# Output-weight pieces: gate row kept on chip, split inside the raw tile, one store per piece

## The chip, the cores and the metric

The kernel runs on 1 core of one Trainium2 chip. The metric is the device time of one execution in microseconds (us), as the median of several runs. TensorE (PE) does the matmuls, VectorE (DVE), ScalarE (ACT) and GpSimd (POOL) work beside it, and every transfer of this stage is issued from the queue of SyncE (SP). Each engine, and SP too, takes its instructions strictly in the order in which they stand in its program: one that waits holds up all behind it.

## The reference

One layer of a trunk over 2048 latent positions with 256 context positions, in float32. What the change touches is the weight of the output projection and its gate:

```
ada = jnp.einsum('bd,lde->lbe', jax.nn.silu(c), w_ada) + b_ada[:, None, :]
sh1, sc1, g1, sh2, sc2, g2 = (m[:, None, :] for m in jnp.split(ada[l], 6, axis=-1))
h = modulate(rmsnorm(x, norm_mix[l]), sh1, sc1)
o, _, _ = token_mixers(h @ w_in[l], lb_f, lb_b, first, hf_c, hb_c, *mix_args)
x = x + g1 * (o @ w_out[l])
h2 = modulate(rmsnorm(x, norm_ffn[l]), sh2, sc2)
x = x + g2 * conv_ffn(h2, w_up[l], conv_w[l], conv_b[l], w_down[l], rows)
return rmsnorm(x, norm_final)
```

`w_out` is 1024 x 1024 and `g1` has 1024 elements. The kernel multiplies the columns of `w_out` by `g1` ahead of time, so that the output projection is a plain product. The token mixers are a gated recurrence of 4 heads in two directions and a spatial gate of 4 heads.

## The kernel before

**Stages.** The input projection and the mixers run first, in two halves of 1024 positions each (about 50 to 540 us and 540 to 1000 us of the profiled execution). The output projection and the second norm follow, then the up-projection with its convolution and the down-projection. float32 products are made of three products of rounded halves ("hi" and "lo", type float32r): `split` (line 128) copies a tile to its rounded hi half on ACT (line 131) and subtracts that from the tile on DVE or POOL to get the lo half (line 132).

**Banks of the input projection.** `run_banks` walks over blocks of 128 columns of `w_in`. For each block and each 512 positions, 24 matmuls fill one PSUM bank `pj`. The block's weights come in by `load_raw` (line 213, 512 KB into a `raw` tile), ACT casts them to `whi`, and POOL (or DVE) subtracts to `wlo`. The inputs are `xh` and `xl`. At the middle, between the two halves, 16 loads of 512 KB (lines 1048 and 1049) bring in the second half's `xh` and `xl`, each as soon as PE has last read the piece that it overwrites. The first three blocks of the second half are called here the first block (the recurrence's output gate, evicted through `sig` and `sgt`), the second block (values, evicted to `vv`) and the third block (queries, evicted through `sig` and `qs`).

**Heads.** The work of a head runs beside the next head's banks: DVE makes `Q` (line 758), POOL makes `kd` (755), PE makes the scores `sc` (line 65), then seven levels follow each other, each with a masked copy (781), an update of `Q` (481), of the keys `K` on DVE and POOL (557) with copies on ACT (559), and of the totals `tot` (488).

**Output weights.** `w_out_ops` (lines 917 to 932) is a generator in a queue of background work. `Pump` steps it when a rough count of PE time has passed what it yielded, so the yields space its pieces: 5.0 between a piece's loads and its arithmetic, 2.5 after its stores. There are 16 pieces of 128 x 512. Each takes a `raw` tile of 128 x 1024: the weight goes into its first half (line 924), the gate's row, broadcast to 128 partitions, into its second (line 925). DVE multiplies (928), ACT casts to the hi half in a tile `wo_hi` of its own, of which there is one (`acc`, shared with other work), DVE subtracts into the half that held the gate, and two transfers store hi and lo to `wo_d` in HBM (930, 931). `raw` has 3 buffers, which these pieces share with `load_raw` and, later, with `w_down_ops`.

**Order.** Outside a few stretches a scheduler (Tile) places the instructions on each engine's queue by its own estimate of when each can run; `pin` keeps an instruction at its place in the order in which the program was written.

Of the kernel before, what the change touches and what calls it, by code (L numbers as in the profile page):

```python
# [9 lines left out]
F32 = mybir.dt.float32  # L10
F32R = mybir.dt.float32r
# [7 lines left out]
P = 128  # L19
D = 1024  # L20
NK = D // P
# [62 lines left out]
def tile_trunk(ctx, tc, x, c, cx, c_ctx, w_ada, b_ada, norm_mix, norm_ffn, w_in, hg_norm, sgu_g, sgu_b,  # L84
               w_sp, b_sp, w_out, w_up, conv_w, conv_b, w_down, norm_final, masks, out):
    nc = tc.nc
    V, S, G, T = nc.vector, nc.scalar, nc.gpsimd, Tensor(nc.tensor)
    ld = nc.sync.dma_start
    st = nc.sync.dma_start
    pin = tc.keep_in_program_order  # L90
# [22 lines left out]
    g_d = dr.tile([2, D], F32, name="g_d")  # L113
# [3 lines left out]
    wo_d = dr.tile([P, NK, 2, D], F32, name="wo_d")  # L117
# [11 lines left out]
    def split(hi, lo, raw, eng=None, keep=lambda i: i):  # L129

        keep(S.copy(hi, raw))  # L131
        (eng or G).tensor_sub(lo, raw, hi.bitcast(F32))  # L132
# [56 lines left out]
    with es1:  # L189
        ps = es1.enter_context(tc.tile_pool(name="ps1", bufs=1, space=PSUM, reuse_waits="tile"))  # L190
        p1 = es1.enter_context(tc.tile_pool(name="p1", bufs=1, reuse_waits="tile"))
        pm = es1.enter_context(tc.tile_pool(name="pm", bufs=1, reuse_waits="tile"))
# [13 lines left out]
        def raw_tile():  # L206
            return p1.tile([P, D], F32, tag="raw", name="raw", bufs=3)
# [52 lines left out]
        acc = ph.tile([P, 2, 512], F32, tag="S", name="acc")  # L260
# [655 lines left out]

        def w_out_ops():

            for k in range(NK):
                for n in range(2):  # L920
                    cl = slice(n * 512, n * 512 + 512)
                    raw = raw_tile()
                    w, g = raw[:, :512], raw[:, 512:]
                    ld(w, w_out[k * P:(k + 1) * P, cl])
                    ld(g, g_d[0:1, cl].broadcast_to([P, 512]))
                    yield 5.0
                    hi = pm.tile([P, 512], F32, tag="acc", name="wo_hi")
                    V.tensor_mul(w, w, g)
                    split(hi.bitcast(F32R), g.bitcast(F32R), w, V)
                    st(wo_d[:, k, 0, cl], hi)  # L930
                    st(wo_d[:, k, 1, cl], g)
                    yield 2.5

        def w_down_ops():
# [20 lines left out]
        def head(hh, h):  # L955
# [18 lines left out]
            def pre_g():  # L974
                if prev[0] >= 0:
                    need(hg_q, (prev[0], prev[1], "keys"))
                else:
                    need(bg_q, "x1")
                    for e in range(8):
                        bg_q.add(ada_block(e))  # L980
                    bg_q.add(w_out_ops())
                    bg_q.add(conv_taps())
                    bg_q.add(w_down_ops())
                t["F"] = pk.tile([P, 2, TH], F32, tag="F", name="F", align_bytes=AL)
                t["K"] = pk.tile([P, 2, TH], F32, tag="K", name="K", bufs=2, align_bytes=AL)
# [130 lines left out]
    def ubank():  # L1116
        return ps2.tile([P, 512], F32, tag="up", name="up", bufs=4)
# [363 lines left out]
    for n, (u, i) in enumerate(prods):  # L1481
# [4 lines left out]
        p = ubank()  # L1486
        hi, lo = u.A[i]
# [34 lines left out]
    V = Kept(nc.vector, pin)  # L1522
# [243 lines left out]
```

## Time and profile before

| what | before |
|---|---|
| median of 3 runs | 2491.28 us (2486.34 to 2496.11) |
| profiled execution, its own time | 2488.51 us |
| its span from first to last instruction | 2486.7 us |
| mean granted PE clock | 0.996 |
| busy share of the span: PE / DVE / ACT / POOL | 97% / 72% / 39% / 43% |
| mean DMA rate over the span | 161 GB/s |

Times in the text are microseconds from the start of the span. A row of the timeline has the start, the duration, the engine, the line, the operation, `out<-in`, and in brackets how long the engine sat idle before it and what ended that. Instructions that follow each other and are alike are merged into one row with their count.

### The profile page before, as it was taken

The page shows a single profiled execution, that of the slowest core. Times are in us where ns is not written, and L with a number is a line of the kernel's source. Part 1 is how long each engine was busy: PE and PEld are TensorE (multiplying, and loading weights), DVE is VectorE, ACT ScalarE, POOL GpSimd, SP SyncE. Part 2 cuts the span into 40 slices and gives each one's busy share as a digit, 9 for nine tenths or more (in the row PEclk, how much of TensorE's full clock was granted, in tenths as well). Part 3 has the DMA queues.
Part 4 walks back from the last instruction along what each step waited for, and adds up shares of the span by engine and source line. Part 5 has one row for each costly group of instructions (what it writes and reads, how often), then busy time and mean ns, then how long its engine had stood idle before and what let it go on. Part 6 is the DMA issues. An engine that isn't in the chain of part 4 may idle for free.

```text
span 2486.7 us, 32820 instructions
## 1 busy us (share of the span) xinstructions
PE 2423.9 (97%) x11859; PEld 2014.4 (81%) x11859; DVE 1793.6 (72%) x2375; ACT 963.8 (39%) x1607; POOL 1059.7 (43%) x871
## 2 busy tenths in 40 slices
PE   7999999999999999999999999999999999999998
PEld 4787888788888888788778888878878888888887
DVE  5866875646765856465699778759999993685876
ACT  2554334433344443245443333324333342433343
POOL 1444232232333433100587887878878770000002
PEclk9999999999999999999999999999999999999999
DMA  8355445573353422768832222372222239834745
GB/s 296 97 189 188 126 138 188 175 261 115 106 179 127 148 98 86 241 207 260 299 103 91 89 87 90 132 282 84 84 86 91 91 100 349 306 126 149 228 148 195
DMA packets 307838, 400.13 MB, mean 161 GB/s; under 512 B 33105, under 2 KB 216137, under 8 KB 304605
## 3 DMA queue, kind: packets, MB, share of 16 engines
q1 hardware_dynamic: 304420, 397.30, 47.9%
q8 instruction: 94, 1.54, 0.3%
q10 hardware_dynamic: 3257, 0.75, 0.1%
q14 instruction: 67, 0.55, 0.1%
HBM read 288.85 MB, written 109.13 MB: 160 GB/s over the span
## 4 chain that ended last, share of the span: by engine, by line
PE 38%; DVE 7%; issue 3%; ACT 1%; POOL 1%; DMA 1%; SPq 0%; POOLq 0%; ACTq 0%; DVEq 0%
PE up L65 24%; PE dn L65 14%; DVE dn L1343 3%; DVE edges L1348 1%; DVE gp L1419 1%; ACT dn L1340 0%; DMA yf<-yd 0%; POOL ra L1625 0%; POOL rr L1626 0%; POOL Al L132 0%; DVE keep L1413 0%; DMA xn<-cv 0%; DVE keep L1429 0%; ACT cv L1362 0%; ACT Ah L131 0%
## 5 line engine op out<-in xcount | busy, mean ns | idle before, releaser
L1343 DVE SCALAR_TENSOR_TENSOR dn<-gp,taps,dn 128x1024 f32<-128x1024 f32 x352 | 448.9, 1282 | 21.0 <-ACT dn L1340 17.8
L65 PE MATMUL up<-yf,Ah 128*128 128x512 f32 x1232 | 394.7, 390 | 2.7 <-DMA yf<-yd 2.7
L132 POOL TENSOR_TENSOR Al<-raw,Ah 128x512 fp32r<-128x512 f32 x264 | 344.4, 1313 | 92.6 <-ACT Ah L131 87.5
L65 PE MATMUL dn<-thl,mhl 128*128 128x512 f32 x1680 | 381.5, 390 | 1.2 <-ACT thl L131 1.2
L65 PEld LDWEIGHTS dn<-thl,mhl 128*128 128x128 f32 x1680 | 315.3, 188 | 67.4 <-ACT thl L131 2.0
L65 PE MATMUL pj<-xh,whi 128*128 128x512 f32 x896 | 364.9, 408 | 0.5 <-ACT xh L131 0.5
L65 PE MATMUL pj<-xl,whi 128*128 128x512 f32 x896 | 351.7, 393 | 1.9 <-DVE xl L132 1.1
L65 PE MATMUL pj<-xh,wlo 128*128 128x512 f32 x896 | 351.7, 393 | 1.0 <-DVE wlo L132 1.0
L65 PE MATMUL up<-xah,Al 128*128 128x512 f32 x704 | 275.9, 392 | 2.0 <-POOL Al L132 1.8
L65 PE MATMUL up<-xah,Ah 128*128 128x512 f32 x704 | 275.5, 391 | 1.8 <-ACT Ah L131 1.8
L65 PEld LDWEIGHTS up<-yf,Ah 128*128 128x128 f32 x1232 | 231.7, 188 | 51.3 <-DMA yf<-yd 3.5
L131 ACT CAST Ah<-raw 128x512 fp32r<-128x512 f32 x264 | 160.5, 618 | 285.3 <-PE up L65 214.6
L132 POOL TENSOR_TENSOR wlo<-raw,whi 128x1024 fp32r<-128x1024 f32 x56 | 135.6, 2421 | 253.1 <-ACT whi L131 222.8
L65 PE MATMUL up<-xal,Ah 128*128 128x512 f32 x528 | 205.9, 390 | 0.0
L65 PE MATMUL up<-yf,Al 128*128 128x512 f32 x528 | 205.5, 389 | 0.0
L65 PEld LDWEIGHTS pj<-xh,wlo 128*128 128x128 f32 x896 | 168.7, 188 | 37.0 <-DVE wlo L132 1.7
L65 PEld LDWEIGHTS pj<-xh,whi 128*128 128x128 f32 x896 | 169.4, 189 | 33.9 <-issue 3.5
L65 PEld LDWEIGHTS pj<-xl,whi 128*128 128x128 f32 x896 | 169.5, 189 | 33.5 <-DVE xl L132 2.1
L65 PE MATMUL dn<-wo,o 128*128 128x512 f32 x768 | 183.2, 395 | 1.5 <-DVE nt L684 0.9
L65 PEld LDWEIGHTS dn<-wo,o 128*128 128x128 f32 x768 | 142.0, 188 | 31.3 <-issue 1.1
L65 PEld LDWEIGHTS up<-xah,Al 128*128 128x128 f32 x704 | 132.6, 188 | 32.8 <-POOL Al L132 5.2
L1625 POOL TENSOR_SCALAR ra<-ss 128x1 f32<-128x1 f32 x8 | 5.2, 661 | 359.0 <-ACT jk L1617 359.0
(311 smaller groups left out, 4201.2 us busy)
## 6 DMA issues: line engine op xcount, KB each, us to landing
raw<-in_w_up_dram SPq DMA_DIRECT2D x88, 512.0 KB
mr<-m SPq DMA_DIRECT2D x85, 512.0 KB
raw<-in_w_in_dram SPq DMA_DIRECT2D x68, 512.0 KB
sT<-wd SPq DMA_DIRECT2D x88, 256.0 KB
raw<-in_w_ada_dram SPq DMA_DIRECT2D x32, 512.0 KB
yf<-yd SPq DMA_DIRECT2D x14, 1024.0 KB
m<-cv SPq DMA_DIRECT2D x22, 544.0 KB
raw<-in_w_down_dram SPq DMA_DIRECT2D x22, 512.0 KB
```

The costliest lines, as they stand in the source:

```text
L65: return self.engine.matmul(out, lhsT, rhs, **kw)
L131: keep(S.copy(hi, raw))
L132: (eng or G).tensor_sub(lo, raw, hi.bitcast(F32))
L1343: V.scalar_tensor_tensor(out=cr, in0=gt[:, t // 3:t // 3 + RH, t % 3:t % 3 + GW], scalar=taps[:, t * NF + f:t * NF + f + 1], in1=cr, op0=A ...
L1348: V.scalar_tensor_tensor(out=e[:, 0, :], in0=gt[:, 1, t % 3:t % 3 + GW], scalar=taps[:, t * NF + f:t * NF + f + 1], in1=e[:, 0, :], op0=AL ...
L1419: V.tensor_add(g_rows(hh, f + c, n2), quad(p, kind), quad(add, kind))
L1625: G.tensor_scalar(out=a, in0=ss, scalar1=plus, scalar2=None, op0=ALU.add)
```

## The change

For each half of the columns, the gate's row is now loaded once, into a tile of `acc` (named `g1`), and stays there for eight pieces. A piece loads its weight into the second half of its `raw` tile, multiplies it there, casts to the first half and subtracts in place in the second half; one transfer of 512 KB then stores both. The multiply and the cast are kept in written order. The yield between load and arithmetic is 6.0 instead of 5.0, and the pieces now run over all eight row blocks of one half of the columns before the other half. The number of gate loads falls from 16 to 2, the number of stores from 32 to 16.

```diff
-            for k in range(NK):
-                for n in range(2):
-                    cl = slice(n * 512, n * 512 + 512)
+            for n in range(2):
+                cl = slice(n * 512, n * 512 + 512)
+                g = pm.tile([P, 512], F32, tag="acc", name="g1")
+                ld(g, g_d[0:1, cl].broadcast_to([P, 512]))
+                for k in range(NK):
                     raw = raw_tile()
-                    w, g = raw[:, :512], raw[:, 512:]
+                    hi, w = raw[:, :512], raw[:, 512:]
                     ld(w, w_out[k * P:(k + 1) * P, cl])
-                    ld(g, g_d[0:1, cl].broadcast_to([P, 512]))
-                    yield 5.0
-                    hi = pm.tile([P, 512], F32, tag="acc", name="wo_hi")
-                    V.tensor_mul(w, w, g)
-                    split(hi.bitcast(F32R), g.bitcast(F32R), w, V)
-                    st(wo_d[:, k, 0, cl], hi)
-                    st(wo_d[:, k, 1, cl], g)
+                    yield 6.0
+                    pin(V.tensor_mul(w, w, g))
+                    split(hi.bitcast(F32R), w.bitcast(F32R), w, V, pin)
+                    st(wo_d[:, k, :, cl], raw.rearrange("p (w c) -> p w c", w=2))
                     yield 2.5
```

The order of PE's instructions is the same in both kernels except in the first three blocks of the second half, and that of POOL except for one swap there. On DVE, ACT and SP it differs from the first piece on.

DVE, where the third head of the first half begins (`Q<-qs,F` opens it, `L928` is a piece's multiply, `L132` with `raw` its subtraction). Before:

```order
L928 TENSOR_TENSOR raw<-raw 128x512
L758 TENSOR_TENSOR Q<-qs,F 128x1024
L132 TENSOR_TENSOR raw<-raw,wo_hi 128x512
L928 TENSOR_TENSOR raw<-raw 128x512
L758 TENSOR_TENSOR Q<-qs,F 128x1024
L557 TENSOR_TENSOR K_3783<-K,F 128x256x2
L132 TENSOR_TENSOR raw<-raw,wo_hi 128x512
L952 SCALAR_TENSOR_TENSOR sgt<-pj,sig 128x512
L928 TENSOR_TENSOR raw<-raw 128x512
L132 TENSOR_TENSOR raw<-raw,wo_hi 128x512
L488 TENSOR_TENSOR tot<-F 128x1024
```

And after:

```order
L928 TENSOR_TENSOR raw<-raw,g_3445 128x512
L758 TENSOR_TENSOR Q<-qs,F 128x1024
L132 TENSOR_TENSOR raw<-raw 128x512
L928 TENSOR_TENSOR raw<-raw,g_3445 128x512
L758 TENSOR_TENSOR Q<-qs,F 128x1024
L132 TENSOR_TENSOR raw<-raw 128x512
L557 TENSOR_TENSOR K_3763<-K,F 128x256x2
L951 SCALAR_TENSOR_TENSOR sgt<-pj,sig 128x512
L488 TENSOR_TENSOR tot<-F 128x1024
L928 TENSOR_TENSOR raw<-raw,g_3445 128x512
```

The multiply ahead of the first `Q` is the fifth piece's before and the third piece's now, and none stands any more between `sgt` and `tot`.

SP at the middle (`L213` loads a block of `w_in`; `xl`, `xh` are the second half's inputs). Before, from the last piece's store:

```order
L931 DMA wo_d_81<-raw_4514 128x512
L939 DMA g2_4704<-g_d_76 128x512
L213 DMA raw_4535<-in_w_in_dram 128x8x128
L653 DMA oT0_77<-nt_4263 128x512
L213 DMA raw_4623<-in_w_in_dram 128x8x128
L465 DMA tr_4656<-in_conv_w_dram 99x128
L1049 DMA xl_347<-xl_d_80 128x2x512
L1048 DMA xh_348<-xh_d_79 128x2x512 x2
```

And after, the start of the 16 loads of `xl` and `xh`:

```order
L213 DMA raw_4428<-in_w_in_dram 128x8x128
L465 DMA tr_4719<-in_conv_w_dram 99x128
L1048 DMA xl_347<-xl_d_80 128x2x512
L1047 DMA xh_348<-xh_d_79 128x2x512
L930 DMA wo_d_81<-raw_4327 128x2x512
L1047 DMA xh_348<-xh_d_79 128x2x512
L1048 DMA xl_347<-xl_d_80 128x2x512
L930 DMA wo_d_81<-raw_4384 128x2x512
L926 DMA raw_4441<-in_w_out_dram 128x512
```

And after, from the last of the 16:

```order
L1048 DMA xl_347<-xl_d_80 128x2x512
L213 DMA raw_4481<-in_w_in_dram 128x8x128
L926 DMA raw_4518<-in_w_out_dram 128x512
L213 DMA raw_4571<-in_w_in_dram 128x8x128
L930 DMA wo_d_81<-raw_4441 128x2x512
L930 DMA wo_d_81<-raw_4518 128x2x512
```

Between these two pieces the other twelve loads of `xl` and `xh` follow each other. `raw_4535` and `raw_4623` hold the second and the third block of the second half before, and both were loaded ahead of the 16 loads; `raw_4481` and `raw_4571` hold them now, and both stand behind. `raw_4571` takes the buffer of `raw_4481`, so its load waits until POOL has subtracted that block.

ACT at the same place, from the end of the first half's last bank (`F<-pj`). Before:

```order
L131 CAST whi_4537<-raw_4535 128x1024
L532 ACTIVATE F_4368<-pj_4481 128x512
L537 ACTIVATE K_4369<-pj_4481 128x256x2
L951 ACTIVATE sig_4571<-pj_4541 128x512
L766 COPY sc_4590<-sc_4591 128x512
L766 COPY sc_4590<-sc_4597 128x512
L131 CAST whi_4625<-raw_4623 128x1024
L951 ACTIVATE sig_4620<-pj_4580 128x512
L559 COPY K2_4646<-K_4369 128x256x2 x2
```

And after:

```order
L950 ACTIVATE sig_4523<-pj_4487 128x512
L766 COPY sc_4536<-sc_4537 128x512
L766 COPY sc_4536<-sc_4543 128x512
L950 ACTIVATE sig_4568<-pj_4526 128x512
L131 CAST whi_4483<-raw_4481 128x1024
L131 CAST raw_4441<-raw_4441 128x512
L131 CAST raw_4518<-raw_4518 128x512
L131 CAST whi_4573<-raw_4571 128x1024
L559 COPY K2_4594<-K_4330 128x256x2
L566 COPY vv_4624<-pj_4577 128x512
L559 COPY K2_4594<-K_4330 128x256x2
```

The cast of the second block (`whi_4537`, now `whi_4483`) stood ahead of the first block's evictions and now stands behind both; the cast of the third block (`whi_4625`, now `whi_4573`) is still ahead of the first copies of the keys `K2`, and POOL's subtraction for it is still ahead of POOL's half of these keys.

## Rows read from the trace of the kernel before

**Rows 1.** The page, part 1: PE's busy time, share and instructions.
```profile
PE 2423.9 (97%) x11859; PEld 2014.4 (81%) x11859; DVE 1793.6 (72%) x2375; ACT 963.8 (39%) x1607; POOL 1059.7 (43%) x871
```

**Rows 2.** Timeline of PE, 425 to 600 us: rows with idle time before them.
```profile
431.87 2.05 PE L65 MATMUL sc<-qs,kd 128*128 128x128 f32 x16 [0.99 <-POOL kd L755]
...
439.67 2.92 PE L65 MATMUL sc<-Q,K 128*128 128x128 f32 x16 [1.62 <-ACT sc L766]
448.56 2.19 PE L65 MATMUL sc<-Q,K 128*128 128x128 f32 x16 [1.20 <-ACT K L559]
...
453.33 0.95 PE L69 MATMUL mi<-ident,vv 128*128 128x128 f32 x4 [1.87 <-ACT vv L566]
...
486.38 2.02 PE L65 MATMUL sc<-Q,K 128*128 128x128 f32 x16 [1.28 <-DVE Q L481]
...
501.79 1.16 PE L65 MATMUL mi<-vt,kt 128*128 128x128 f32 x8 [1.27 <-ACT fs L810]
...
564.41 0.66 PE L69 MATMUL mi<-ident,vv 128*128 128x128 f32 x4 [0.95 <-ACT vv L566]
```

**Rows 3.** Timeline of DVE, 385 to 530 us: multiplies of pieces that came late.
```profile
424.71 0.69 DVE L928 TENSOR_TENSOR raw<-raw 128x512 f32<-128x512 f32 x1 [10.25 <-DMA raw<-g_d]
...
437.75 0.69 DVE L928 TENSOR_TENSOR raw<-raw 128x512 f32<-128x512 f32 x1 [2.00 <-DMA raw<-g_d]
...
450.62 1.53 DVE L928 TENSOR_TENSOR raw<-raw 128x512 f32<-128x512 f32 x1 [0.18 <-issue]
...
481.75 0.69 DVE L928 TENSOR_TENSOR raw<-raw 128x512 f32<-128x512 f32 x1 [4.43 <-DMA raw<-g_d]
...
499.86 0.69 DVE L928 TENSOR_TENSOR raw<-raw 128x512 f32<-128x512 f32 x1 [4.10 <-DMA raw<-g_d]
```

**Rows 4.** Timeline of ACT, the same stretch: casts of pieces, and what stood behind them.
```profile
438.52 0.62 ACT L131 CAST wo_hi<-raw 128x512 fp32r<-128x512 f32 x1 [4.96 <-DVE raw L928]
439.04 1.06 ACT L766 COPY sc<-sc 128x512 f32<-128x512 f32 x2
...
452.19 0.61 ACT L131 CAST wo_hi<-raw 128x512 fp32r<-128x512 f32 x1
452.70 0.58 ACT L566 COPY vv<-pj 128x512 f32<-128x512 f32 x1
```

**Rows 5.** Timeline of SP, the same stretch: the gate load that DVE awaited at 481.75.
```profile
478.00 0.42 SPq L925 DMA_DIRECT2D raw<-g_d  x1
```

**Rows 6.** Stretches of 2 us: busy PE, PEld, DVE, ACT, POOL; PE clock, DMA share, GB/s.
```profile
452.00:454.00 2.00, 0.67 (x5) 0.67 (x5) 1.33 (x3) 1.28 (x3) 0.00 (x0) 0.89 0.17 68
454.00:456.00 2.00, 2.00 (x7) 1.61 (x6) 2.00 (x4) 1.09 (x2) 0.00 (x0) 0.50 0.52 195
456.00:458.00 2.00, 2.00 (x8) 1.57 (x8) 1.41 (x3) 0.63 (x2) 0.79 (x1) 0.76 0.70 204
```

**Rows 7.** Timeline of SP at the middle: second and third block, last `xl`, next block.
```profile
521.09 0.38 SPq L213 DMA_DIRECT2D raw<-in_w_in_dram  x1
...
523.39 0.39 SPq L213 DMA_DIRECT2D raw<-in_w_in_dram  x1
...
541.22 0.54 SPq L1049 DMA_DIRECT2D xl<-xl_d  x1
```

**Rows 8.** One stretch of 3 us at the middle, columns as in Rows 6.
```profile
536.00:539.00 3.00, 3.00 (x15) 2.50 (x14) 2.47 (x1) 0.41 (x1) 1.39 (x1) 1.00 1.05 408
```

**Rows 9.** Timeline of ACT at the middle.
```profile
552.88 1.04 ACT L131 CAST whi<-raw 128x1024 fp32r<-128x1024 f32 x1 [3.35 <-PE pj L65]
553.83 0.59 ACT L951 ACTIVATE sig<-pj 128x512 f32<-128x512 f32 x1
554.32 1.20 ACT L559 COPY K<-K 128x512 f32<-128x512 f32 x1
```

**Rows 10.** Timeline of POOL at the middle: second block's subtraction, and the keys' first level.
```profile
540.42 2.41 POOL L132 TENSOR_TENSOR wlo<-raw,whi 128x1024 fp32r<-128x1024 f32 x1 [3.03 <-ACT whi L131]
...
556.35 1.91 POOL L557 TENSOR_TENSOR K<-K,F 128x512 f32<-128x512 f32 x1
```

**Rows 11.** Timeline of PE at the middle: two matmuls of a bank that follow each other.
```profile
541.76 0.39 PE L65 MATMUL pj<-xh,wlo 128*128 128x512 f32 x1
541.99 0.39 PE L65 MATMUL pj<-xh,whi 128*128 128x512 f32 x1
```

## The prediction

> **What bounds the kernel now.** I read the page's busy shares first: PE is busy for 2423.9 us, 97% of the span [rows 1]. Whatever is done for the other engines can thus give back only PE's idle time, and only where PE idles for the thing that is changed. So I went to PE's own timeline in the stretch in which the 16 pieces run, 388 to 519 us, and a little past it. There are six gaps, 0.99, 1.62, 1.20, 1.87, 1.28 and 1.27 us, together 8.23 us [rows 2]. None of them names the output weights; each names an engine that feeds the heads. The timelines of DVE and ACT tell what held those engines. DVE stood for 10.25, 2.00, 4.43 and 4.10 us in front of a piece's multiply that waited for the gate's row [rows 3]. ACT stood behind DVE: the cast of a piece waited 4.96 us for a multiply, and the copy `sc` for which PE idled until 439.67 came right behind that cast; the copy `vv` for which PE idled until 453.33 likewise came right behind a cast, whose multiply had taken 1.53 us instead of 0.69 [rows 2 to 4]. DVE's 4.43 us stands 4 us ahead of the gap that names `Q`, its 4.10 us right ahead of the one that names `fs`. So all six are shadows of the pieces, cast through engines that work in order.
>
> One more cost of these gaps is no gap: from 452 to 458 us the granted clock reads 0.89, 0.50 and 0.76 [rows 6], so PE sat for a while at 1.2 instead of 2.4 GHz after idling 1.33 of the 2 us from 452 on. The loss is 2 x (0.11 + 0.50 + 0.24) = 1.7 us. In all the stretch has 8.23 + 1.7 = 9.9 us to give, 0.4% of the time. A difference of 0.5%, 12.5 us, is about what a measurement of this kernel can tell from no change.
>
> **What the change takes away.** DVE's in-order queue no longer meets a multiply whose operand was asked for late: 14 of 16 gate loads are gone, and the diff's yields put 6.0 instead of 5.0 between load and multiply. A load of 256 KB took 478.00 to 481.75, 3.75 us, from its issue to the waiting multiply [rows 3, 5]; the new order issues the third to tenth piece's loads at least that far ahead of their multiplies, and a multiply no longer stands between `sgt` and `tot`. I take away the gaps of 1.62, 1.20, 1.87, 1.28 and 1.27 us, 7.24 us. I leave the first, 0.99: `kd` there stands behind a weight block's subtraction on POOL, and that block's own load still comes after the previous block's. What is late next I read from the head in the middle, which has no output pieces beside it: it still has a gap of 0.95 us for `vv` [rows 2]. So the likeliest gain is 7.24 - 0.95 = 6.3 us, with the clock's 1.7 us 8.0 us. The bounds are half of that, 4.0 us, if loads that now wait for a 512 KB store are late in their turn, and 9.9 us, everything.
>
> **Edits that cost nothing.** DVE's two operations and ACT's cast per piece keep their shapes (0.69 and 0.62 us [rows 3, 4]). Writing hi and lo inside the raw tile ends the wait for the one `wo_hi` tile, but ACT's idle time there is no path of its own. Thirty fewer issues at 0.42 us [rows 5] free SP for 12.6 us, during which nobody waited for SP but the pieces. If the cover of PE's own matmuls were gone, the 16 x 0.69 x 2 us of DVE would count; they count the same in both kernels.
>
> **What the change moves, and what that costs.** 16 pieces at 8.5 instead of 7.5 last 16 us longer, so the last of them now run into the middle, where SP issues the 16 loads of `xl` and `xh`. The order shows the price. Before, the second and third block of the second half were loaded at 521.09 and 523.39, ahead of the 16 loads [rows 7]. Now pieces hold two of the three raw buffers there: the second block's load stands behind the last `xl` (541.22 [rows 7]), and the third block's needs the second's buffer. Call E the end of the first block's second bank. ACT now casts the second block behind that bank's eviction, which holds ACT 554.32 - 553.83 = 0.49 us, and the cast takes 1.04 [rows 9]. PE can start the second block at E + 1.53: a gap of 1.5 us. It has four matmuls that need no lo half, 0.23 us each [rows 11], then waits for POOL's subtraction of 2.41 us [rows 10], done at E + 3.94: a gap of 1.5 us. Only then may the third block be loaded. Its 512 KB take the 3.75 us of a 256 KB load and 0.26 MB more at 408 GB/s [rows 8], 0.64: landed at E + 8.3, cast by E + 9.4. Behind this cast on ACT stand one copy of `K` (0.60, half of the merged 1.20 [rows 9]) and that of `vv` (0.58 [rows 4]): E + 10.6, while PE, 26 matmuls further, is there at E + 9.9: a gap of 0.7 us. POOL subtracts the third block by E + 11.8 and only then forms its half of the first keys, 1.91 [rows 10], and ACT copies that: E + 14.3. PE, after the transposes of `vv` (0.66 [rows 2]) and a matmul, wants the scores at E + 11.5: a gap of 2.8 us. Together 6.5 us, in place of the 0.95 us before: 5.5 us lost. Idling 6.5 us within 15 us is at least what the gaps until 439.67, 448.56 and 453.33 made (4.7 us in 15), which ended in 1.7 us at the low clock; I count 1.7 again. The loss is 7.2 us, with bounds of 2.1 (the third block lands in time, no clock) and 12.1, as below.
>
> The Trainium skill prices a transfer lower: its page "DMA: Bandwidth & Descriptors", section "Anatomy of one DMA — SWDGE (gpsimd) path", fits about 2.0 us and the bytes at 436 GB/s, for a path other than the hardware queues that the profile shows here. By it the third block's 512 KB land in 3.2 instead of 4.4 us (an estimate from that page); the fourth gap shrinks by 1.2 us, and the sum would be 1.2 us lower. The rows have 3.75 us for half the bytes, so I keep mine.
>
> The 16 loads get company too: two stores of 0.52 MB and a load of 0.26 MB stand among them, 1.31 MB, which at 408 GB/s [rows 8] is 3.2 us for a queue that ran full there. Part of PE's cover is new: the first scores now stand inside that bank, so PE reaches the last `xl` about 2 us later. I take 0 and keep 3.2 us for the range.
>
> Outside these stretches PE's order is the same, and the down weights that follow come 16 us later into a stretch in which PE hardly idles: 0, with 2 us either way for the range.
>
> **The sum.** -8.0 + 7.2 = -0.8 us. The profiled execution took 2488.51 us, 2.8 us less than the median of 2491.28, well inside the spread of the three runs (2486.34 to 2496.11). From the profile's own time the sum is 2487.7; on the median's scale 2490.5.
>
> **Rivals.** *The middle is cheap* (chance 0.21). The third block lands and is cast before anyone stands behind it, and the clock holds: then only the two gaps of 1.5 us are left there, less 0.95: -8.0 + 2.1 = -5.9, 2485 us. For it: 408 GB/s empties the queue soon after the last `xl`. Against it: buffers and order, not bandwidth, put that load behind POOL's subtraction.
>
> *The middle costs more than the pieces gave* (0.15; the other side). One mechanism: SP holds the second half of the `xl` and `xh` loads behind a piece's store, which waits for DVE, which waits for ACT's cast behind a bank's eviction. The last `xl` then lands 3.2 us later, and if PE comes to it first, PE pays that on top and drops the clock once more: -8.0 + 7.2 + 3.2 + 1.7 = +4.1, 2495 us. It decides from the point where the last `xl` lands after PE has reached that bank's last two steps.
>
> *The change doesn't do what it says* (0.08). The loads are late still, because each now waits until a 512 KB store out of the same buffer has landed: half the gain, -4.0 + 7.2 = +3.2, 2494 us.
>
> **Chances.** The likeliest, gain and loss that cancel, has 0.56 and gives 2490 us. The Trainium skill (page "TensorE: Matmul & The Clock Gate", Part 1) names idling as what takes the clock to its low level; rows 6 agree, and that moved the clock's 1.7 us into the likeliest case. With the bounds of gain (4.0 to 9.9) and loss, 2 us either way and a spread of runs of some 4 us, the range is 2480 to 2499 us. Beyond 12.5 us either way there is no mechanism with a price from these rows: all that PE idles here is 9.9 us. I leave 0.06 for faster and 0.08 for slower, which has the rival beyond its price and unknown prices behind it; 0.86 for within 0.5%.
>
> **What would show it.** In the profile after, from 425 to 510 us: no multiply of a piece on DVE idles for a DMA by more than 1 us, PE's gaps there fall to 1 to 2 us, the clock reads 1.00 throughout. From 545 to 575 us: a gap of PE for `whi` on ACT, one for `wlo` on POOL, and one for the first scores, each of 1.5 to 3 us, and a stretch below full clock. If the first set of gaps stays, the reading of DVE's waits is wrong; if the second is missing, the reading of the order in the middle is. A gap that names `xl` would speak for the rival on the slow side.

## The result and the profile after

The changed kernel takes 2493.13 us (median of 20 runs) where the one before takes 2490.08 (20 runs): a ratio of 1.0014, 95% interval 1.0008 to 1.0020, so 2 to 5 us slower. Two further measurements gave 1.0013 (1.0004 to 1.0021) and 1.0011 (1.0001 to 1.0020). The prediction had -0.8 us. The loss is real, though under the 12.5 us that the prediction took for what can be told from no change; the sign of the sum was wrong.

The profiled execution took 2490.77 us, its span is 2488.9. PE is busy as before [rows 1]:

```profile
PE 2428.3 (98%) x11859; PEld 2016.1 (81%) x11859; DVE 1801.7 (72%) x2375; ACT 964.7 (39%) x1607; POOL 1060.4 (43%) x871
```

PE's timeline, rows that answer to [rows 2], the pieces' stretch first, then the middle, then one row behind both:

```profile
434.42 2.05 PE L65 MATMUL sc<-qs,kd 128*128 128x128 f32 x16 [1.22 <-POOL kd L755]
451.95 0.66 PE L69 MATMUL mi<-ident,vv 128*128 128x128 f32 x4 [1.32 <-ACT vv L566]
...
547.93 0.50 PE L65 MATMUL pj<-xl,whi 128*128 128x512 f32 x1 [0.22 <-DMA xl<-xl_d]
550.97 0.50 PE L65 MATMUL pj<-xh,whi 128*128 128x512 f32 x1 [1.62 <-ACT whi L131]
553.59 0.50 PE L65 MATMUL pj<-xh,wlo 128*128 128x512 f32 x1 [1.42 <-POOL wlo L132]
560.51 0.66 PE L69 MATMUL mi<-ident,vv 128*128 128x128 f32 x4 [0.72 <-ACT vv L566]
564.48 3.15 PE L65 MATMUL sc<-Q,K 128*128 128x128 f32 x16 [3.08 <-ACT K L559]
...
648.73 0.66 PE L69 MATMUL mi<-ident,vv 128*128 128x128 f32 x4 [1.23 <-ACT vv L566]
```

Six gaps of 8.23 us in the pieces' stretch have become two of 2.54. In the middle one gap of 0.95 has become five of 7.06, and four of them are those that the prediction worked out as 1.5, 1.5, 0.7 and 2.8 us. The last row was not foreseen: the gap for `vv` one head later is 1.23 us now. In PE's timeline before it was 0.47:

```profile
645.45 0.66 PE L69 MATMUL mi<-ident,vv 128*128 128x128 f32 x4 [0.47 <-ACT vv L566]
```

DVE's timeline, multiplies of pieces, against [rows 3]: none has idle time before it any more.

```profile
425.29 0.68 DVE L928 TENSOR_TENSOR raw<-raw,g 128x512 f32<-128x512 f32 x1
437.72 0.68 DVE L928 TENSOR_TENSOR raw<-raw,g 128x512 f32<-128x512 f32 x1
448.86 0.67 DVE L928 TENSOR_TENSOR raw<-raw,g 128x512 f32<-128x512 f32 x1
```

The middle, first SP, then POOL, then ACT (their timelines): the third block's load leaves as POOL ends the second block's subtraction (551.05 + 2.48 = 553.53), is cast 4.4 us after its issue, and the keys follow behind the third block on POOL and on ACT.

```profile
553.56 0.37 SPq L213 DMA_DIRECT2D raw<-in_w_in_dram  x1
...
551.05 2.48 POOL L132 TENSOR_TENSOR wlo<-raw,whi 128x1024 fp32r<-128x1024 f32 x1 [13.48 <-ACT whi L131]
559.11 2.37 POOL L132 TENSOR_TENSOR wlo<-raw,whi 128x1024 fp32r<-128x1024 f32 x1 [5.58 <-ACT whi L131]
561.44 1.81 POOL L557 TENSOR_TENSOR K<-K,F 128x512 f32<-128x512 f32 x1
...
557.93 1.05 ACT L131 CAST whi<-raw 128x1024 fp32r<-128x1024 f32 x1 [5.91 <-DMA raw<-in_w_in_dram]
563.28 1.15 ACT L559 COPY K<-K 128x512 f32<-128x512 f32 x1 [2.82 <-POOL K L557]
```

The clock, in stretches of 2 us as in [rows 6]: PE does nothing from 562 to 564, and then the granted clock is low as it was at 452 to 458 before. 2 x (0.18 + 0.50 + 0.18) = 1.7 us: a spell of the same size, in another place.

```profile
562.00:564.00 2.00, 0.00 (x0) 0.00 (x0) 0.00 (x0) 0.72 (x1) 1.25 (x1) 1.00 0.57 154
564.00:566.00 2.00, 1.52 (x10) 1.52 (x11) 1.54 (x3) 1.54 (x3) 0.05 (x1) 0.82 0.97 331
566.00:568.00 2.00, 2.00 (x10) 1.90 (x10) 1.34 (x3) 0.46 (x1) 1.51 (x1) 0.50 0.21 80
568.00:570.00 2.00, 2.00 (x9) 1.59 (x8) 2.00 (x3) 0.72 (x2) 0.00 (x0) 0.82 0.24 90
```

**How the kernels are compared below.** Four evictions on ACT, the same in every kernel, serve as marks: ahead of the first changed instruction that matters, at the end of the pieces' stretch, behind the middle, and one head further. In ACT's timeline after they stand at

```profile
390.25 0.60 ACT L657 ACTIVATE gu<-pj 128x512 f32<-128x512 f32 x1
...
501.74 0.60 ACT L657 ACTIVATE gu<-pj 128x512 f32<-128x512 f32 x1 [3.69 <-PE pj L65]
...
604.13 0.60 ACT L532 ACTIVATE F<-pj 128x512 f32<-128x512 f32 x1 [2.15 <-PE pj L65]
...
678.22 0.60 ACT L662 ACTIVATE gv<-pj 128x512 f32<-128x512 f32 x1 [1.61 <-PE pj L65]
```

and before at 387.97, 507.75, 601.61 and 674.90. Their differences are the lengths of three stretches: the pieces', the middle's and the next head's. The three stretches are read from one profile each where no number of profiles is given. The last column is measured over 11 to 20 runs beside runs of the kernel before. Each profile is one execution, so the sum of three stretches and the ratio need not agree to the microsecond.

| kernel | pieces | middle | next head | sum against before | ratio (95% interval) |
|---|---|---|---|---|---|
| before, mean of 4 profiles | 118.9 (117.4 to 119.8) | 93.7 | 73.3 | 0 | e1_same 0.9996 (0.9987 to 1.0005) |
| after, mean of 3 | 111.6 | 102.3 | 74.1 | +2.0 | 1.0014, 1.0013, 1.0011 |
| e2_early | 116.6 | 97.5 | 74.1 | +2.2 | 1.0012 (1.0004 to 1.0021) |
| e3_late | 118.9 | 97.7 | 74.1 | +4.7 | 1.0010 (1.0001 to 1.0018) |
| e4_nopin | 115.3 | 98.8 | 74.1 | +2.2 | 1.0012 (1.0003 to 1.0021) |
| e5_pause | 111.6 | 93.5 | 73.6 | -7.3 | 0.9979 (0.9970 to 0.9988) |
| e7_down | 111.5 | 100.8 | 73.3 | -0.4 | 1.0011 (1.0003 to 1.0020) |
| e8_gate16 | 111.6 | 105.2 | 74.1 | +4.9 | 1.0020 (1.0011 to 1.0029) |
| e12_pin | 113.6 | 103.1 | 73.3 | +4.1 | 1.0009 (1.0000 to 1.0018) |

### The profile page after: what moved, and what is told of

Its sections match the earlier page's. It is cut to its first block, busy times and chain, and to the rows that moved or that the text cites. A ratio compares the mean times of both kernels' runs of the same rounds, so it can differ in the third digit from the quotient of the medians.

```text
span 2488.9 us, 32776 instructions
## 1 busy us (share of the span) xinstructions
PE 2428.3 (98%) x11859; PEld 2016.1 (81%) x11859; DVE 1801.7 (72%) x2375; ACT 964.7 (39%) x1607; POOL 1060.4 (43%) x871
## 3 DMA queue, kind: packets, MB, share of 16 engines
q8 instruction: 94, 1.54, 0.3%
## 4 chain that ended last, share of the span: by engine, by line
PE 38%; DVE 6%; issue 3%; POOL 1%; ACT 1%; DMA 1%; POOLq 0%; SPq 0%; ACTq 0%; DVEq 0%
PE up L65 24%; PE dn L65 14%; DVE dn L1342 3%; DVE edges L1347 1%; DVE gp L1418 1%; ACT dn L1339 0%; DMA yf<-yd 0%; POOL Al L132 0%; POOL ra L1624 0%; POOL rr L1625 0%; DVE keep L1412 0%; DMA xn<-cv 0%; DVE keep L1428 0%; ACT cv L1361 0%; POOL raw L1168 0%
## 5 line engine op out<-in xcount | busy, mean ns | idle before, releaser
L132 POOL TENSOR_TENSOR Al<-raw,Ah 128x512 fp32r<-128x512 f32 x264 | 343.8, 1310 | 90.7 <-ACT Ah L131 77.5
L132 POOL TENSOR_TENSOR wlo<-raw,whi 128x1024 fp32r<-128x1024 f32 x56 | 137.4, 2454 | 256.2 <-ACT whi L131 242.1
```

## The experiments

Theory M, formed from the two traces: the gain in the pieces' stretch and the loss in the middle are separate, and the loss comes from the second and third block's loads, which stand behind the 16 loads of `xl` and `xh`. Its rivals differ from run to run and stand in the expectations.

**The same two kernels again** (e1, e9, e10: before; e6, e11: after). In the first pair of profiles the changed kernel was already 2.3 us late at the first mark, ahead of any instruction that differs. Either that is scatter, or it belongs to the program.

> The kernel before, once more, as a control. Both theories: ratio 1.000 within 0.001. The profile tells whether the 2.3 us by which the changed kernel's profile was late at 390 us, ahead of any changed instruction, is scatter from run to run (then this control differs from the first profile of before by as much, one way or the other, at the same place) or belongs to the changed program (then this control agrees with the first profile within 0.5 us up to 390 us).

> The changed kernel once more, on the same chip as the others of this set. Theory M with scatter ahead of 390 us: the ratio to before is 1.0005 to 1.0015 (1.2 us from PE's gaps between 390 and 670 us, and chance for the rest); the profile's lateness at 390 us, 2.3 us in the first profile, is another number, and its difference from before between 390 and 670 us is again +1 to +2 us. Rival (the changed program itself is slower ahead of 390 us): again 2 us late at 390 us.

> The kernel before, a third profile, for the time at which work that both kernels have in the same order is done at 390 us. So far two profiles of before agree there within 0.2 us, while six of seven profiles of kernels with the changed pieces are 1.0 to 4.0 us late there and one 0.4 us. Theory S (scatter: how many spells at the low clock fall into the first 390 us is chance): this profile is off by a spell, 1.7 us, or part of one in either direction as easily as not. Theory G (it goes with the program): within 0.5 us of the other two.

> The kernel before, a fourth profile, as the one ahead of it. Theory S: at least one of the two is off by 1 us or more at 390 us. Theory G: both are within 0.5 us.

> The changed kernel, a third profile and a third measurement of the ratio. Between 390 and 670 us +1 to +2 us against before by both theories. At 390 us, theory S: anything from 0 to 4 us late; theory G: 1 to 2.5 us late, as in the two other profiles of this same program (2.3 and 1.0). Ratio 1.0005 to 1.0020.

The first mark stood at 387.97, 387.95, 389.81 and 388.35 in the four profiles of before, at 390.25, 388.94 and 388.14 in the three of after. Loss at the low clock in the first 390 us, as 10 x (1 - clock) summed over stretches of 10 us, is 5.1, 5.1, 8.6 and 6.8 us in the one and 8.6, 6.8 and 5.1 in the other: in these seven profiles the mark follows the spells, in both programs. After e1 it looked as if it went with the program, e9 (1.8 us later than its twin) and e11 (0.2 later than the first profile of before) undid that: it is scatter. The three stretches, in contrast, repeat better: the middle of after is 102.1 to 102.4 us long in all three profiles, that of before 93.6 to 93.9. (e7, which has the same order of work up to 640 us, has 100.8; see there.) The pieces' stretch of before is less steady, 117.4 to 119.8. This is what lets a loss of 2 us in 2490 be traced at all.

**The pieces ahead of the middle, set closer** (e2).

```
-                    yield 6.0          # load to multiply
+                    yield 4.0
...
-                    yield 2.5          # behind the store
+                    yield 2.0
```

> The changed kernel with its pieces set closer: 4.0 in place of 6.0 between load and arithmetic, 2.0 in place of 2.5 behind the store, so that all pieces end ahead of the middle and both blocks' loads stand ahead of the 16 loads of xl and xh again, as before. Theory M (the whole loss sits in the middle and comes from those two loads standing behind the last xl): the loss of 8.5 us goes, the gain of 8 us stays or shrinks to 5 where a load is late again; 5 to 8 us faster than before, some 2483 us, and PE's gaps between 545 and 570 us are the one of 1 us for vv again. Theory L (the loss comes with what the pieces do to the program elsewhere, the middle's gaps replaced others that were hidden): at most 2 us faster than before.

Some 3 us slower (1 to 5 by the interval) instead of 5 to 8 faster; by the expectation's own bounds this is the outcome of theory L, not of theory M. Both blocks' loads do stand ahead of the 16 (519.81 and 521.49), the gaps of 1.62 and 1.42 for `whi` and `wlo` are gone, and yet the middle is 3.8 us longer and the pieces' gain has shrunk to 2.3. PE's timeline has gaps for `K` in both places (and one of 1.07 us in the middle for another load, `tr`, at 527.85):

```profile
449.69 2.19 PE L65 MATMUL sc<-Q,K 128*128 128x128 f32 x16 [2.06 <-ACT K L559]
454.98 0.85 PE L69 MATMUL mi<-ident,vv 128*128 128x128 f32 x4 [2.38 <-ACT vv L566]
...
564.24 3.56 PE L65 MATMUL sc<-Q,K 128*128 128x128 f32 x16 [2.01 <-ACT K L559]
```

Their cause is on POOL and DVE. At the first, the timelines of the two engines in e2:

```profile
444.68 3.78 POOL L557 TENSOR_TENSOR K<-K,F 128x512 f32<-128x512 f32 x1
...
444.63 2.21 DVE L481 TENSOR_TENSOR Q<-Q,F 128x1024 f32<-128x1024 f32 x1
```

and in the changed kernel at the same work:

```profile
443.19 1.95 POOL L557 TENSOR_TENSOR K<-K,F 128x512 f32<-128x512 f32 x1
...
443.90 3.33 DVE L481 TENSOR_TENSOR Q<-Q,F 128x1024 f32<-128x1024 f32 x1
```

Whichever of the two starts first runs at its own speed (POOL 1.95, DVE 2.21) and the other stands until it is done: 444.63 + 2.21 + 1.95 is 448.8 against 448.46 measured, 443.19 + 1.95 + 2.21 is 447.4 against 447.23. In e2 DVE won by 0.05 us, the keys came 1.8 us later, and PE waited. In the middle POOL's `K` comes second as well and takes 3.79, but by more than a hair: DVE's `Q` stands ready at 557.12, while POOL subtracts the third block until 559.2. That block's cast now stands behind the first block's second `sig` on ACT (555.74 behind 555.24), where before it stood ahead of it [rows 9]. So the closer spacing did what it was made for and changed who comes first elsewhere. The kernel before lost the same race in the pieces' stretch, and won it in the middle by 0.02 us (556.35 [rows 10] against DVE at 556.37); its four profiles agree, with 3.84 to 3.85 us for `K` at the first place and 1.90 to 1.92 at the second:

```profile
443.48 3.85 POOL L557 TENSOR_TENSOR K<-K,F 128x512 f32<-128x512 f32 x1
...
443.45 2.21 DVE L481 TENSOR_TENSOR Q<-Q,F 128x1024 f32<-128x1024 f32 x1
...
556.37 3.99 DVE L481 TENSOR_TENSOR Q<-Q,F 128x1024 f32<-128x1024 f32 x1
```

The Trainium skill states this as a rule (page "SBUF — State Buffer", section "Who interferes with whom"): a DVE instruction with two inputs in SBUF and a POOL instruction that reads SBUF share a port, and the first to start keeps it for its whole length. The sums above agree with it.

**The kernel before with its pieces pushed into the middle** (e3).

```
                     ld(g, g_d[0:1, cl].broadcast_to([P, 512]))
-                    yield 5.0
+                    yield 6.0
```

> The kernel before with one number changed: 6.0 in place of 5.0 between a piece's loads and its arithmetic, so that its pieces run into the middle as in the changed kernel and both blocks' loads stand behind the last xl; gate loads, two stores and wo_hi are as before. Theory M: the middle costs what it cost in the changed kernel, 6.5 us of gaps and the clock, so about 5.5 to 8.5 us are lost there; the longer lead takes part of DVE's late multiplies away, up to 4 us; in all 2 to 8 us slower than before. Theory L: no more than 1 us slower. PE's gaps between 545 and 570 us would be near 1.5, 1.5, 0.7 and 3 us by M, one of 1 us by L.

0.2 to 4.5 us slower: in the range of theory M, though the ratio alone does not exclude the 1 us of theory L, and of the four gaps that M named one is there. The lead alone leaves the pieces' stretch as long as it was: multiplies still wait for gate rows (3.13 us at 459.07). The middle is 4.0 us longer, with the gap for the scores,

```profile
563.47 3.34 PE L65 MATMUL sc<-Q,K 128*128 128x128 f32 x16 [3.01 <-ACT K L559]
```

and a low spell of 1.7 us, but without those for `whi` and `wlo`: here the second block's load was issued at 513.64, ahead of the 16, and cast at 539.05. Only the third block's stands behind them (543.82, the last `xl` at 540.24), and its cast waits for it until 554.40, 1.5 us later than before. POOL then subtracts until 557.9, and its `K` comes behind DVE's `Q` (timelines of POOL and DVE):

```profile
557.89 4.34 POOL L557 TENSOR_TENSOR K<-K,F 128x512 f32<-128x512 f32 x1
...
556.36 3.66 DVE L481 TENSOR_TENSOR Q<-Q,F 128x1024 f32<-128x1024 f32 x1
```

Counted from the second mark the keys start 1.8 us later than before and take 2.4 us longer. So the position of the pieces costs the middle without any other edit, but here by one late load and the race that it makes POOL lose, not by the gaps of the changed kernel.

**The changed kernel without its pins** (e4).

```
-                    pin(V.tensor_mul(w, w, g))
-                    split(hi.bitcast(F32R), w.bitcast(F32R), w, V, pin)
+                    V.tensor_mul(w, w, g)
+                    split(hi.bitcast(F32R), w.bitcast(F32R), w, V)
```

> The changed kernel without the two pins: the scheduler places a piece's multiply and cast by its own estimate. The loads of both blocks still stand behind the last xl. Theory M: the middle's loss is the same, 8 us. If the pins make the gain (multiplies placed behind work that is due earlier), up to half of the 8 us gained between 425 and 510 us is lost, 2 to 4 us slower than the changed kernel; if the row that stays on chip and the single store make it, within 1 us of the changed kernel.

The gain in the pieces' stretch falls from 7.4 to 3.7 us: half of it goes with the pins. The scheduler sets a multiply early, and it then waits for its own weight, in DVE's timeline for instance

```profile
424.50 1.46 DVE L928 TENSOR_TENSOR raw<-raw,g 128x512 f32<-128x512 f32 x1 [6.99 <-DMA raw<-in_w_out_dram]
```

and 5.38 us at 444.91, after which PE idles 2.04 us for `Q`. The middle loses 5.1 us here, with a single gap of 4.12 for the scores. Against the expectation the second block's load stands ahead of the 16 (512.12), only the third block's behind them (540.27), and the race is lost as in e3: POOL's `K`, at 558.10, takes 4.31 us. What the middle gives back covers what the pieces' stretch loses, and the ratio, 1.0012, is that of the changed kernel.

**The gate's row loaded 16 times again** (e8).

```
-                g = pm.tile([P, 512], F32, tag="acc", name="g1")   # ahead of the loop over k
-                ld(g, g_d[0:1, cl].broadcast_to([P, 512]))
                 for k in range(NK):
...
                     ld(w, w_out[k * P:(k + 1) * P, cl])
+                    g = pm.tile([P, 512], F32, tag="acc", name="g1")
+                    ld(g, g_d[0:1, cl].broadcast_to([P, 512]))
```

> The changed kernel, but with the gate's row loaded for every piece again (16 loads into the tile g1, each behind its weight's load), the rest as changed: split inside the raw tile, one store, two pins, 6.0 between load and multiply. If it is the later place of the multiply (lead and pins) that gives the gain: no multiply waits for a gate's row by more than 1 us, PE's gaps between 425 and 510 us stay at 2.5 us, within 1 us of the changed kernel. If the row that stays on chip gives it: multiplies wait for DMA again by 2 to 10 us, and up to half of the 8 us gained there goes, 2 to 4 us slower than the changed kernel.

The pieces' stretch is 111.6 us long, as in the changed kernel: the row that stays on chip is worth nothing there, and two multiplies that wait 1.97 and 1.05 us for it cost nothing. But the whole is 3 to 7 us slower than before, and 2.3 us slower than the changed kernel measured beside it (2493.38 against 2491.11): the middle is 2.9 us longer than the changed kernel's, and PE now waits for `xl` three times there:

```profile
537.91 0.50 PE L65 MATMUL pj<-xl,whi 128*128 128x512 f32 x1 [0.90 <-DMA xl<-xl_d]
540.44 0.50 PE L65 MATMUL pj<-xl,whi 128*128 128x512 f32 x1 [0.75 <-DMA xl<-xl_d]
551.64 0.50 PE L65 MATMUL pj<-xl,whi 128*128 128x512 f32 x1 [0.79 <-DMA xl<-xl_d]
```

This is close to the mechanism of the prediction's rival on the slow side, brought about by the gate loads among the 16: SP issued a piece's store at 525.71 us and then stood until 529.83 ahead of a piece's load, 3.7 us of it for a piece's store to land, with thirteen loads of `xl` and `xh` behind it. In the changed kernel itself the wait for `xl` is 0.22 us, 0.18 and 0.74 in its three profiles.

**The pins alone** (e12).

```
-                    V.tensor_mul(w, w, g)
-                    split(hi.bitcast(F32R), g.bitcast(F32R), w, V)
+                    pin(V.tensor_mul(w, w, g))
+                    split(hi.bitcast(F32R), g.bitcast(F32R), w, V, pin)
```

> The kernel before with the two pins alone (multiply and cast of a piece keep their written order); 16 gate loads, two stores, wo_hi and the yield of 5.0 are as before. In the order the pieces end somewhat later: the second block's load stands behind the first of the 16 loads of xl and xh, the third block's behind the last. If the pins give the gain: no multiply of a piece idles for DMA by more than 2 us, PE's gaps between 425 and 510 us fall from 8.2 to 2 to 4 us, 4 to 7 us earlier at 510 us; the third block then costs 2 to 5 us in the middle, and the whole is 0 to 4 us faster than before. If the pins do little and the change's other edits (the row on chip, the lead of 6.0, the one store) are what gives the gain: gaps there of 6 to 8 us as before, and the whole 2 to 5 us slower than before.

The pins do give most of the gain: no multiply waits for more than 0.47 us, and the pieces' stretch is 5.4 us shorter with gate loads, two stores and `wo_hi` as before. What is left of gaps is one of 2.45 for `K`, the race again (POOL 3.76), and 0.71. The middle, though, loses 9.4 us instead of 2 to 5: 2.12 and 0.75 for `xl`, 1.62 and 0.64 for the second block, and 5.1 us at the low clock. The whole is 0 to 4.5 us slower than before, where the pins were to make it 0 to 4 faster.

**One multiply of the down weights moved** (e7).

```
-                    yield 9.0
+                    yield 11.0 if (n, j) == (0, 4) else 9.0
```

> The changed kernel with one number changed for one piece of the down weights: its yield ahead of the multiply is 11 in place of 9, by which that multiply goes on DVE from its place behind the first halved total (at 645 us, beside POOL's subtraction of keys, which took 2.04 instead of 1.30 us there) to the place behind the next, where it stands in the kernel before. Theory P (POOL was slowed by the multiply beside it, and vv's copy came late for that): POOL's 2.04 us are 1.3 again, PE's gap at 649 us falls from 1.23 to 0.5 us, 0.75 us faster than the changed kernel from there on. Rival (the delay comes from ahead of it): the gap stays at 1.2 us.

Theory P holds. POOL and DVE in the changed kernel (L943 is the down weights' multiply), then POOL and PE in e7 (timelines):

```profile
645.48 2.04 POOL L557 TENSOR_TENSOR K<-K,tot 128x512 f32<-128x512 f32 x1 [3.47 <-ACT K L559]
...
645.14 1.20 DVE L943 TENSOR_TENSOR raw<-raw,g 128x1024 f32<-128x1024 f32 x1
```

```profile
643.90 1.30 POOL L557 TENSOR_TENSOR K<-K,tot 128x512 f32<-128x512 f32 x1 [3.47 <-ACT K L559]
...
646.41 0.66 PE L69 MATMUL mi<-ident,vv 128*128 128x128 f32 x4 [0.48 <-ACT vv L566]
```

POOL is back at 1.30, the gap at 0.48, the next head at 73.3 us. It is the same port: 645.14 + 1.20 + 1.30 is 647.64, against 647.52 measured. The 0.8 us are too few for the ratio to show (1.0011 against 1.0013). The -0.4 in the table is not theirs: up to 640 us the engines' order is that of the changed kernel, and the middle is 1.6 us shorter in an execution in which the low clock fell at 552 to 560, ahead of the wait for the scores (which is 1.54 us there instead of 3.08), and not behind it.

**The changed kernel with its pieces parted by the middle** (e5).

```
                 for k in range(NK):
+                    if n == 1 and k == 3:
+                        yield 45.0
                     raw = raw_tile()
```

> The changed kernel with one pause: ahead of the twelfth of the 16 pieces the generator yields 45, so that eleven pieces run ahead of the middle at the changed kernel's own spacing, and five behind it; both blocks' loads stand ahead of the 16 loads of xl and xh again. Theory M (gain of 8 us in the pieces' stretch, loss of 8.5 us in the middle, which comes from those two loads alone): the gain stays, the middle has the one gap of 1 us for vv, and at 645 us the down weights' multiply stands where it stood before (no 0.8 us): 6 to 8 us faster than before, some 2482 us. Theory L (pieces cost as much wherever they stand, so five pieces behind the middle make gaps there): PE's gaps reappear between 560 and 620 us, and the kernel is within 2 us of before.

2483.59 us against 2488.97: a ratio of 0.9979 (0.9970 to 0.9988), 3 to 7.5 us faster than before, the fastest of all kernels here. PE's timeline has the changed kernel's two gaps in the pieces' stretch, and those of the kernel before behind it:

```profile
432.66 2.05 PE L65 MATMUL sc<-qs,kd 128*128 128x128 f32 x16 [1.35 <-POOL kd L755]
450.20 0.66 PE L69 MATMUL mi<-ident,vv 128*128 128x128 f32 x4 [1.32 <-ACT vv L566]
...
556.26 0.66 PE L69 MATMUL mi<-ident,vv 128*128 128x128 f32 x4 [0.88 <-ACT vv L566]
...
637.60 0.66 PE L69 MATMUL mi<-ident,vv 128*128 128x128 f32 x4 [0.48 <-ACT vv L566]
```

The second and third block were loaded ahead of the `xl` and `xh`, all of the gain stays (111.6), nothing is lost in the middle (93.5), and five pieces behind the middle make no gap. Of theory M this stands: gain and loss are separate, and the loss hangs on where the pieces stand. That it comes from the two blocks' late loads alone does not: in e2, e3 and e4 with none or one of them late the middle is 3.8 to 5.1 us longer, and each time POOL's `K` comes behind DVE's `Q`. In e5 POOL is first again, by 0.03 us (548.32 against 548.35).

## Why the prediction was wrong: two large terms that nearly cancel, and three that were each off to the same side

The steps were right in the main; the sum, -0.8 us, was smaller than what its terms were off by, and so its sign hung on them. The term furthest off is the loss in the middle.

**The gain** was sized well: -8.0 forecast, 118.9 to 111.6 us measured, -7.4. In the first pair of profiles, 8.3 us apart, the idle rows fall by 5.7 us, the clock's 1.7 us go, and 0.9 us are in neither; what is left is 1.22 and 1.32 us where 0.99 and 0.95 were forecast. In e10 the same six gaps (7.4 us) brought no low spell, and its stretch is 117.4 us long: the clock's 1.7 us stand in three of the four profiles of before. One reading behind the gain was incomplete. The gap of 1.20 for `K` at 448.56 [rows 2] was put down to pieces in ACT's and DVE's queues; POOL's 3.85 us at 443.48, twice its 1.91 [rows 10], show the race. The multiply's 1.53 us at 450.62 [rows 3] are the same thing from the other side: POOL's `K` ran from 450.09 for 1.51 us. That this gap went is in part luck: e2 and e12, in which no multiply waits for more than 0.47 us from 425 on either, lost the race by 0.05 and 0.04 us and kept gaps of 2.06 and 2.45 for `K`. And of the edits it is the pins, not the row on chip, that carry most of the gain (e4, e8, e12): the prediction named the later place of the multiply, but as one reason among three.

**The loss in the middle** had its mechanism right and its size wrong, and it is the step that failed by most: 7.2 forecast, 93.7 to 102.3 measured, +8.6. The gaps went as the text had them, one by one (1.62, 1.42, 0.72 and 3.08 for 1.5, 1.5, 0.7 and 2.8), the load took 4.37 us where 4.39 was worked out, and the clock lost its 1.7. The Trainium skill's fit for another path (page "DMA: Bandwidth & Descriptors", section "Anatomy of one DMA — SWDGE (gpsimd) path"), which the prediction set beside it as an estimate, gave 3.2 us. By the prediction's own times that lower price would have taken the third gap away first and 0.5 us off the fourth; the 1.2 us in all is right. Net of the 0.95 us that was there, the idle rows cost 6.1 us and the clock 1.7, together 7.8, against 5.5 + 1.7: 0.2 us of it is a wait for `xl`, which the prediction had put at 0. The further 0.8 us are in no idle row, but PE's starts show them: three of the gaps stand in the stream of the banks' matmuls, and such a gap costs more than its row says.

```profile
548.97 0.39 PE L65 MATMUL pj<-xh,wlo 128*128 128x512 f32 x1
550.97 0.50 PE L65 MATMUL pj<-xh,whi 128*128 128x512 f32 x1 [1.62 <-ACT whi L131]
551.31 0.39 PE L65 MATMUL pj<-xl,whi 128*128 128x512 f32 x1
```

From the first start to the third are 2.34 us, where two steps of 0.23 [rows 11] take 0.46: 1.88 us lost, 1.62 of them in the row. In the same way the gap for `wlo` costs 1.68 instead of 1.42 and that for `xl` 0.48 instead of 0.22, 0.8 us more for the three. In the third profile of after (e11) the split is another: behind a wait for `xl` the first block's `sig` comes 1.5 us later (38.7 us from the second mark instead of 37.2), and the low clock, 3.4 us, falls ahead of the wait for the scores, which is only 1.19. e7 has the second without the first. So that the three middles of after agree to 0.3 us is in part chance, and one execution's loss can be 7.1 us instead of 8.6.

**What comes later, "0, with 2 us either way"**, is the step that failed by its mechanism, if by less. The prediction put the term at 0 because PE hardly idles there, and did not ask what a moved multiply would stand beside. The down weights come later (their first load at 561.97 instead of 542.54, 19 us where 16 were worked out; the last piece's own multiply stands at 565.67 instead of 516.21), and one multiply of theirs then stands beside POOL's keys: +0.8 us, in e7 undone alone.

With the measured terms the sum is -7.4 + 8.6 + 0.8 = +2.0 in place of -0.8: 1.4 us from the middle, 0.8 from what comes later, 0.6 from the gain. Of the ratio's 2 to 5 us that leaves up to 3 us, which no run here places; the spells outside the three stretches scatter by as much from one execution to the next.

**The rivals.** "The middle costs more" came true by its sum, not by its mechanism: waits for `xl` are 0.2 to 0.7 us long (the 0.7 in e11, with 1.5 us lost behind it), not 3.2; in e8 and e12 they are 2.4 and 2.9. "The middle is cheap" and "doesn't do what it says" fell. The forecast of what the profile would show was met in the main: no multiply waited, the clock was full in the pieces' stretch and low for a while in the middle, and the three named gaps came. PE's gaps in the pieces' stretch fell to 2.5 us, though, not to 1 to 2, and the sign of the slow rival, a gap that names `xl`, was there with 0.2 us.

## What to carry to other kernels

Background work that is respaced ends elsewhere: look in the order for what its last pieces hold (here buffers) when a burst of other loads starts, and part it there; one pause turned 3 us lost into 5 gained. When a large local gain and a large local loss cancel, forecast them as two numbers, and give the sum the errors of both: its sign is no forecast while it is smaller than these. Look for an instruction that takes twice as long at one place as at another: moving work by a few microseconds decided here who comes first of DVE and POOL, and that took 0.7 to 2.4 us more of POOL each time.

## What the runs showed of the hardware that was not expected

- DVE and POOL, each with two inputs in SBUF, do not share the time: one stands until the other is done. POOL's `K` takes 1.9 us or 3.8 to 4.3, by who starts first. In the kernel before the middle's race was won by 0.02 us, and with the same winner in all four of its profiles.
- A gap in the stream of the banks' matmuls cost PE 0.26 us more than its idle row says (1.88 us for 1.62, 1.68 for 1.42, 0.48 for 0.22).
- Spells at the low clock come in pieces of about 1.7 us of loss, and not at the same places in each execution: the first 390 us of one and the same program lost 5.1, 5.1, 6.8 and 8.6 us to them. The execution with 8.6 us there took 2494.0 us, the others 2488.2 to 2489.2, so the spells make part of the scatter. In the pieces' stretch of before, gaps of 7.3 to 8.3 us brought a spell in three executions and none in the fourth.
